# Grouped-query attention on one core: the first K and Q heads as 32-bit loads on SyncE's and ScalarE's queues, GpSimd's correction from job 0 on

## The chip, the cores and the metric

The kernel runs on one core of a Trainium2 chip. The metric is the device time of one execution in microseconds. A core has TensorE (PE; its weight loads are listed apart as PEld), VectorE (DVE), ScalarE (ACT), GpSimd (POOL) and SyncE (SP). The engines run side by side, each in the order of its own instruction list, and wait for each other through semaphores. A transfer is issued on the queue of SP, ACT or POOL and moved by 16 DMA engines. TensorE writes to PSUM, from which VectorE and ScalarE read.

## The reference

Q is 8 x 512 x 32 x 64 (batch, sequence, heads, dimension), K and V are 8 x 512 x 8 x 64, all fp32. Four query heads share one K and one V head.

```python
scores = np.einsum('bhqd,bhkd->bhqk', Q, K_expanded) * scale      # scale = 1/sqrt(64)
weights = np.exp(scores - np.max(scores, axis=-1, keepdims=True))
weights = weights / (np.sum(weights, axis=-1, keepdims=True) + 1e-10)
output = np.einsum('bhqk,bhkd->bhqd', weights, V_expanded)
```

## The kernel before

The work is 64 jobs. A *unit* u is one batch and one pair of K heads (32 units, 8 query heads each); a *job* j is one of the two K heads of a unit (g = j % 2) with its four query heads, taken as two pairs i = 0, 1. Two heads of a pair stand in the lower and the upper 64 partitions (m = 0, 1), so one transpose of 128 x 128 turns two heads at once.

Per job the scores are computed transposed, keys in the partitions and the 512 queries along the row, in 16 blocks (i, kc, m). ScalarE takes 14 of them in seven tiles of two (13 in the wide jobs, even ones from 8 on): two matmuls into a PSUM tile `s_ps` (two buffers), then one `activation(Exp)` into `pt` (`act_tile`, L220 to L228). The remaining two blocks (three) go to VectorE through the PSUM tile `d_ps` (one buffer): `u` is the linear part of an exponential made of bits (L237), `f` masks its fraction (L258), `g` and `w` are a correction (`correction`, L248), and the sum of u and w is written into `pt` (`exp_d4`, L268). `by_pool(j)` says who computes g and w: VectorE for jobs 0 to 2 and the last one, GpSimd for the others. Where GpSimd does it, `exp_d4` comes one job later.

While job j's scores run, the output of job j - 1 is computed: 64 matmuls with `pt` as weights into the PSUM tile `pv` (one buffer; `pv`, L287), first pair i = 0, then i = 1. A column of ones in V gives the row sums. VectorE takes the reciprocal and writes `o_sb` (`norm`, L330), which frees `pv`. SyncE stores a unit's output.

Q is loaded by GpSimd's queue, which rounds fp32 to bf16 on the way, into `q_nat` (four buffers). It is transposed on TensorE against an identity (`trans_q`, L165) into `d_ps` and copied to `qt` by VectorE. K of batches 1 to 7 is transposed by DMA (`dma_k`, on SyncE's queue, issued in the code at job 4 of the batch before). K of batch 0 is transposed on TensorE (`first_k`, L136) and copied to `kt_first`. Of each pair of K heads there are two versions, the heads in order and swapped (`swap`), so that each head is at hand in both halves of the partitions. The plain version takes four transposes and the swapped one eight.

The order is written out by hand (`tc.manual_schedule`): each engine executes its instructions in the order of the code. At the start (L395 to L417) GpSimd issues K heads 0 and 1, then Q of unit 0 in three pieces, builds the identity, and issues the rest of batch 0. TensorE runs eight warm-up matmuls, the twelve transposes of K's first pair in both versions into one `d_ps` tile, and then the first Q transposes into the next `d_ps` tile. In every job behind the fourth score tile, TensorE makes the Q transposes for a later job and, in batch 0, those of a later K pair; the copies come behind them on VectorE (`reads`, L463 to L488). At job 1 GpSimd waits for part of job 0's `pt` (`gate`, L429) before it issues the Q loads of units 2 and 3.

Of the kernel before, what the change touches and what calls it, by code (L numbers as in the profile page):

```python
# [11 lines left out]
FP32 = mybir.dt.float32  # L12
BF16 = mybir.dt.bfloat16
# [45 lines left out]
def fast_path(ctx, tc, Q, K, V, out, flag):  # L59
    nc = tc.nc  # L60
    B, S, H, D = Q.shape
    KV = K.shape[2]
    HPG = H // KV
    SC = S // 128
# [8 lines left out]
    const_pool = ctx.enter_context(tc.tile_pool(name="const", bufs=1))  # L73
    qnat_pool = ctx.enter_context(tc.tile_pool(name="qnat", bufs=4))
# [9 lines left out]
    s_pool = ctx.enter_context(tc.tile_pool(name="sps", bufs=2, space=PS))  # L84
    d_pool = ctx.enter_context(tc.tile_pool(name="dps", bufs=1, space=PS))
    pv_pool = ctx.enter_context(tc.tile_pool(name="pv", bufs=1, space=PS))

    ident = const_pool.tile([128, 128], BF16, name="ident")
    ok = const_pool.tile([128, SPB * 2 * SC], FP32, name="ok")
# [4 lines left out]
    ones = const_pool.tile([128, 1], BF16, name="ones")  # L94
    kt_first = const_pool.tile([128, GP, 2, S], BF16, name="kt_first")
    vt = [const_pool.tile([128, SC, KV, D + 1], BF16, name=f"v{j}") for j in range(2)]

    kn, qn, kt, qt = {}, {}, {}, {}

    def load_k(b, lo=0, hi=KV):  # L100
        if b not in kn:
            kn[b] = knat_pool.tile([128, SC, KV, D], BF16, name="k_nat")
        nc.gpsimd.dma_start(
            out=kn[b][:, :, lo:hi, :],
            in_=K[b, :, lo:hi, :].rearrange("(sc p) g d -> p sc g d", p=128),
        )


    def load_v(b, lo=0, hi=KV, chunks=range(SC)):
        for sc in chunks:  # L110
            nc.gpsimd.dma_start(  # L111
                out=vt[b % 2][:, sc, lo:hi, 0:D],
                in_=V[b, sc * 128:(sc + 1) * 128, lo:hi, :],
            )

    def load_v_head(b, g):
        nc.gpsimd.dma_start(
            out=vt[b % 2][:, :, g, 0:D], in_=V[b, :, g, :].rearrange("(sc p) d -> p sc d", p=128)
        )

    def load_q(u, cuts=(0, 2 * HPG)):
        b, gp = divmod(u, GP)
        h0 = gp * 2 * HPG
        qn[u] = qnat_pool.tile([128, SC, 2 * HPG, D], BF16, name="q_nat")
        for lo, hi in zip(cuts[:-1], cuts[1:]):
            nc.gpsimd.dma_start(  # L126
                out=qn[u][:, :, lo:hi, :],
                in_=Q[b, :, h0 + lo:h0 + hi, :].rearrange("(sc p) h d -> p sc h d", p=128),
            )

    def d_tile():
        return d_pool.tile([128, 2, S], FP32, name="d_ps")
# [3 lines left out]
    def first_k(gp, swap, bank):  # L136
        half_bank = bank.bitcast(BF16)[:, 0:S]
        ps = half_bank.rearrange("p (sc c) -> p sc c", sc=SC)
        h = 2 * gp
        for sc in range(SC):  # L140
            if swap:
                for half, g in ((0, 1), (64, 0)):
                    nc.tensor.transpose(ps[half:half + 64, sc, :], kn[0][:, sc, h + g, :], ident)  # L143
            else:
                nc.tensor.transpose(ps[:, sc, :], kn[0][:, sc, h:h + 2, :], ident)  # L145
        return lambda: nc.vector.tensor_copy(out=kt_first[:, gp, swap, :], in_=half_bank)  # L146

    def dma_k(b):
        kt[b] = kt_pool.tile([128, 2, GP, S], BF16, name="kt")
# [39 lines left out]
    NJOB = NU * 2  # L189
    DPAIR = NPAIR - 1  # L190

    def taken(j):
        return 3 if WIDE(j) else 2
# [10 lines left out]
    def scores(j, ps, i, kc, m):  # L204
        u, g = divmod(j, 2)
        b, gp = divmod(u, GP)
        keys = kt_first[:, gp, :, :] if b == 0 else kt[b][:, :, gp, :]
        return nc.tensor.matmul(  # L208
            ps,
            keys[64 * m:64 * m + 64, g ^ m, kc * 128:(kc + 1) * 128],  # L210
            qt[u][64 * m:64 * m + 64, g, i, :],
            start=True,
            stop=True,
        )

    def open_job(j):
        pt = pt_pool.tile([128, NPAIR, SC, 2, S], FP16, name="pt")
        jobs.setdefault(j, {}).update(pt=pt, pv={})

    def act_tile(j, n, spare=None):  # L220
        group = act_tiles(j)[n]
        i, kc, lo = group[0]
        ps = s_pool.tile([128, 2, S], FP32, name="s_ps") if spare is None else spare
        for _, _, m in group:
            scores(j, ps[:, m, :], i, kc, m)
        return nc.scalar.activation(  # L226
            out=jobs[j]["pt"][:, i, kc, lo:, :], in_=ps[:, lo:, :], func=EXP, scale=scale
        )  # L228
# [12 lines left out]


    def by_pool(j):
        return 3 <= j < NJOB - 1

# [16 lines left out]
    def exp_d3(j, engine):  # L264
        st = jobs[j]
        correction(engine, st["f"], st["g"], st["w"])
# [125 lines left out]
        )  # L392


    load_k(0, 0, 2)  # L395
    load_q(0, (0, 2, 4, 8))
    make_identity(nc, ident)
    nc.gpsimd.memset(ones, 1.0)
    nc.gpsimd.memset(ok, 1.0)
    for j in range(2):  # L400
        nc.gpsimd.memset(vt[j][:, :, :, D:D + 1], 1.0)
    load_v_head(0, 0)
    load_k(0, 2, 4)
    load_q(1)
    load_v_head(0, 1)
    load_k(0, 4, KV)
    load_v(0, 2, KV)


    nc.vector.memset(warm, 0.0)  # L410
    bank = d_tile()
    for j in range(8):
        nc.tensor.matmul(bank[:, 1, :], warm[:, 0:128], warm, start=True, stop=True)
    for read in [first_k(0, swap, bank[:, swap, :]) for swap in range(2)]:
        read()
    bank = d_tile()
    trans_q(0, bank[:, 0, :], 0, 1)()  # L417


    for j in range(NJOB):  # L420
        end = j == NJOB - 1
        last = j - 1
        late = last >= 0
        u, g = divmod(j, 2)
        b, gp = divmod(u, GP)
        open_job(j)
        if j == 1:

            nc.gpsimd.tensor_copy(out=gate, in_=jobs[0]["pt"][0:1, 0, SC - 1, 0, 0:1])  # L429
            load_q(2)  # L430
            load_q(3)
        if g == 0 and u >= 1 and u + 3 < NU:
            load_q(u + 3)
        if (gp, g) == (1, 0) and b + 1 < B:
            load_k(b + 1)
        if 3 <= 2 * gp + g < 3 + SC and b + 1 < B:
            load_v(b + 1, chunks=(2 * gp + g - 3,))
        if gp == 2 and g == 0 and b + 1 < B:
            dma_k(b + 1)

        cut = (4, 18) if taken(j) > 2 else (11, 19)
        act_tile(j, 0)
        if j == 0:
            trans_q(0, bank[:, 1, :], 1, NPAIR)()
            act_tile(j, 1)
            exp_d(j, 0, 2, d_tile())()
        else:
            exp_d(j, 0, 2, d_tile())()
            act_tile(j, 1)

        if j == 8:
            check_v(0, 0)
        if g == (b < B - 1) and j > 1:
            check_v(b, gp)
        if late:
            pv(last, 0, 0, 16)
        act_tile(j, 2)
        if late:
            pv(last, 0, 16, 32)
            norm(last, 0)  # L460
        act_tile(j, 3)

        reads = []  # L463
        if not end:
            bank = d_tile()
            beside = act_tile(j, 4, bank) if taken(j) > 2 else None

            ahead = (j + 1,) if j < 6 else (7, 8) if j == 6 else (j + 2,)
            for n, to in enumerate(ahead):
                if to < NJOB:  # L470
                    reads.append(trans_q(to, bank[:, n, :], other=beside))
            if j == 1:
                for swap in range(2):
                    reads.append(first_k(1, swap, bank[:, 1, swap * S // 2:]))
            elif j > 1 and b == 0 and gp + 1 < GP:
                reads.append(first_k(gp + 1, g, bank[:, 1, :]))
        else:
            pv(j, 0, 0, 16)
        copies = [] if by_pool(j) else [read() for read in reads]
        if late and by_pool(last):  # L480
            exp_d4(last)
        check_sums()
        exp_d2(j)
        if not by_pool(j):
            exp_d3(j, nc.vector)
            exp_d4(j)
        else:
            copies = [read() for read in reads]  # L488
        if taken(j) == 2:
            act_tile(j, 4)  # L490
        if late:
            pv(last, 1, 0, cut[0])
        act_tile(j, 5)
        if not end and taken(j + 1) > 2:
            exp_d(j + 1, 2, taken(j + 1), bank[:, 1:2, :], copies[0])()
        if late:
            pv(last, 1, *cut)
        act_tile(j, 6)
        if late:
            pv(last, 1, cut[1], 32)  # L500
            norm(last, 1)
            del jobs[last]
        if end:
            pv(j, 0, 16, 32)
            norm(j, 0)
            pv(j, 1, 0, 32)
            norm(j, 1)
# [118 lines left out]
```

## Time and profile before

| | |
|---|---|
| time, median of 3 runs | 420.73 us (420.61 to 420.81) |
| profiled execution | 421.54 us, of which the span from first to last instruction is 419.8 us |
| ScalarE busy | 401.3 us (96%) |
| TensorE busy | 381.2 us (91%), mean granted clock 0.992 |
| VectorE busy | 345.0 us (82%) |
| GpSimd busy | 293.4 us (70%) |

A timeline row gives the start and the length in us, the engine, the line (L12 is line 12 of the kernel), the operation, what it writes and reads, and how many instructions were merged; in brackets stand the engine's idle time in front and what released it. A group row gives the busy time, the mean of one in ns, and the idle time in front with its releasers. A row of windows gives the busy time of each engine in one stretch.

### The profile page before, as it was taken

What the parts mean: (1) busy time and instruction counts of PE and PEld (TensorE: products, weight loads), DVE (VectorE), ACT (ScalarE), POOL (GpSimd) and SP (SyncE); (2) the same over time, 40 slices, a digit from 0 to 9 for tenths busy, and PEclk for the clock granted to TensorE, in tenths of its full rate; (3) what the DMA queues carried; (4) which work ended last, traced back from release to release, by engine and by line L of the source; (5) the groups of instructions that cost most, each with busy time, mean ns of one, the idle gap of its engine ahead of it and who ended that gap; (6) DMA issues with size and microseconds to landing.
All of it is one profiled execution on the core that took longest, in us unless ns stands there. A gap on an engine that the chain in (4) does not pass through costs nothing.

```text
span 419.8 us, 13065 instructions
## 1 busy us (share of the span) xinstructions
PE 381.2 (91%) x5689; PEld 235.2 (56%) x5689; DVE 345.0 (82%) x612; ACT 401.3 (96%) x449; POOL 293.4 (70%) x209
## 2 busy tenths in 40 slices
PE   7888999999999999999999999999999999999983
PEld 2455565565565556556555556555655655555652
DVE  1687888888888888888888888888889888898875
ACT  2889999999999999999999999999999999999992
POOL 8504757788758876788867887687886887667550
PEclk9899999999999999999999999999999999999998
DMA  9996985599967998499964999659986899732223
GB/s 97 175 143 161 194 188 127 88 204 181 209 152 108 208 198 163 133 205 126 236 145 123 213 152 258 160 77 202 200 178 151 141 189 209 157 115 101 103 101 106
DMA packets 91438, 66.95 MB, mean 159 GB/s; under 512 B 52080, under 2 KB 74608, under 8 KB 91376
## 3 DMA queue, kind: packets, MB, share of 16 engines
q0 software_dynamic: 56544, 25.17, 51.6%
q1 hardware_dynamic: 34832, 40.90, 34.6%
q8 instruction: 45, 0.74, 0.7%
q14 instruction: 17, 0.14, 0.1%
HBM read 50.33 MB, written 33.55 MB: 200 GB/s over the span
## 4 chain that ended last, share of the span: by engine, by line
ACT 80%; PE 12%; DVE 5%; issue 1%; POOL 1%; ACTq 0%; DVEq 0%; POOLq 0%
ACT pt L226 80%; PE s_ps L208 6%; PE pv L302 3%; PE d_ps L172 1%; DVE o_sb L349 1%; DVE pt L271 1%; DVE qt L176 1%; DVE w L254 1%; POOL q_nat L126 0%; DVE u L237 0%; DVE kt_first L146 0%; PE d_ps L143 0%; DVE f L258 0%; DVE g L250 0%; PE d_ps L145 0%
## 5 line engine op out<-in xcount | busy, mean ns | idle before, releaser
L226 ACT ACTIVATE pt<-s_ps 128x1024 f16<-128x1024 f32 x420 | 398.1, 1284 | 9.7 <-PE s_ps L208 9.5
L302 PEld LDWEIGHTS <-pt 128*128 128x128 f16 x4096 | 142.6, 98 | 77.5 <-issue 56.3
L302 PE MATMUL pv<-v,pt 128*128 128x65 bf16 x4032 | 178.8, 195 | 2.4 <-DVE o_sb L349 1.9
L208 PE MATMUL s_ps<-qt,kt 64*128 64x512 bf16 x728 | 142.6, 383 | 22.4 <-ACT pt L226 16.3
L254 POOL TENSOR_TENSOR w<-g,f 128x1024 bf16<-128x1024 bf16 (+1 forms) x60 | 154.7, 2578 | 5.0
L250 POOL TENSOR_SCALAR g<-f 128x1024 bf16<-128x1024 int16 (+1 forms) x60 | 74.5, 1241 | 105.6 <-DVE f L258 105.6
L237 DVE TENSOR_SCALAR u<-d_ps 128x1024 int16<-128x1024 f32 (+1 forms) x92 | 96.8, 1052 | 0.7 <-PE d_ps L208 0.7
L349 DVE TENSOR_TENSOR o_sb<-pv,inv 128x512 f32<-128x512 f32 x125 | 86.4, 691 | 4.3
L208 PEld LDWEIGHTS <-kt 64*128 64x128 bf16 x896 | 51.8, 93 | 62.3 <-issue 35.0
L345 DVE RECIPROCAL inv<-pv 128x8 f32<-128x8 f32 x125 | 25.9, 207 | 54.1 <-PE pv L302 54.1
L271 DVE TENSOR_TENSOR pt<-u,w 128x1536 uint16<-128x1536 int16 (+1 forms) x64 | 51.1, 799 | 0.2
L176 DVE COPY qt<-d_ps 128x1024 bf16<-128x1024 bf16 (+1 forms) x65 | 43.9, 676 | 4.3 <-PE d_ps L172 3.1
L208 PE MATMUL d_ps<-qt,kt 64*128 64x512 bf16 x168 | 43.0, 375 | 0.0
L172 PE MATMUL d_ps<-ident,q_nat 128*128 128x128 bf16 x512 | 40.7, 224 | 1.1 <-DVE kt_first L146 0.9
L172 PEld LDWEIGHTS <-q_nat 128*128 128x128 bf16 x512 | 29.6, 99 | 21.5 <-issue 21.4
L258 DVE TENSOR_SCALAR f<-u 128x1536 int16<-128x1536 int16 (+1 forms) x64 | 30.9, 482 | 0.0
L111 POOL DMA_DIRECT2D v<-in_V_dram x32 | 29.0, 910 | 0.5 <-issue 0.5
L126 POOL DMA_DIRECT2D q_nat<-in_Q_dram x34 | 27.4, 806 | 1.4 <-DMA q_nat<-in_Q_dram 1.2
L208 PE MATMUL s_ps<-qt,kt_first 64*128 64x512 bf16 x112 | 23.4, 413 | 4.5 <-ACT pt L226 3.5
L226 ACT ACTIVATE pt<-d_ps 128x512 f16<-128x512 f32 x28 | 25.2, 899 | 0.0
L182 DVE TENSOR_REDUCE okv<-v 128x1 f32<-128x512 bf16 x32 | 21.6, 675 | 0.0
L208 PEld LDWEIGHTS <-kt_first 64*128 64x128 bf16 x128 | 7.8, 95 | 12.3 <-issue 8.6
(41 smaller groups left out, 45.5 us busy)
## 6 DMA issues: line engine op xcount, KB each, us to landing
out_dram<-o_sb SPq DMA_DIRECT2D x31, 1024.0 KB, 6.5
q_nat<-in_Q_dram POOLq DMA_DIRECT2D x31, 512.0 KB, 5.9
k_nat<-in_K_dram POOLq DMA_DIRECT2D x7, 512.0 KB, 8.3
v<-in_V_dram POOLq DMA_DIRECT2D x28, 128.0 KB, 7.8
kt<-kt SPq DMA_DIRECT2D x14, 256.0 KB, 4.4
out_dram<-o_sb SPq DMA_DIRECT2D x4, 256.0 KB, 2.4
kt<-k_nat SPq DMA_TRANSPOSE x28, 5.7
v<-in_V_dram POOLq DMA_DIRECT2D x4, 96.0 KB, 8.7
```

The costliest lines, as they stand in the source:

```text
L111: nc.gpsimd.dma_start(out=vt[b % 2][:, sc, lo:hi, 0:D], in_=V[b, sc * 128:(sc + 1) * 128, lo:hi, :],)
L172: nc.tensor.transpose(ps[:, i, sc, :], qn[u][:, sc, h:h + 2, :], ident), other
L176: return lambda: apart(nc.vector.tensor_copy(out=qt[u][:, g, lo:hi, :], in_=ps[:, lo:hi, :, :].rearrange("p i sc c -> p i (sc c)")), other)
L208: return nc.tensor.matmul(ps, keys[64 * m:64 * m + 64, g ^ m, kc * 128:(kc + 1) * 128], qt[u][64 * m:64 * m + 64, g, i, :], start=True, st ...
L226: return nc.scalar.activation(out=jobs[j]["pt"][:, i, kc, lo:, :], in_=ps[:, lo:, :], func=EXP, scale=scale)
L237: return lambda: nc.vector.tensor_scalar(out=st["u"][:, lo:hi, :], in0=ps[:, 0:hi - lo, :], scalar1=A_U, scalar2=B_U, op0=ALU.mult, op1=AL ...
L250: engine.tensor_scalar(out=g, in0=f, scalar1=-EXP_F1, scalar2=EXP_K * 2.0 ** (24 * as_bits), op0=ALU.add, op1=ALU.mult,)
L254: engine.tensor_tensor(out=w, in0=g, in1=f.bitcast(FP16) if as_bits else f, op=ALU.mult)
L258: nc.vector.tensor_single_scalar(out=st["f"], in_=st["u"], scalar=1023, op=ALU.bitwise_and)
L271: nc.vector.tensor_tensor(out=st["pt"][:, DPAIR, :, :, :].rearrange("p kc m q -> p (kc m) q")[:, 0:n, :].bitcast(U16), in0=st["u"], in1=st ...
L302: nc.tensor.matmul(st["pv"][i][:, m, qc, :], st["pt"][:, i, kc, m, qc * 128:(qc + 1) * 128], vt[b % 2][:, kc, 2 * gp + g, :], start=(n < 2 ...
L349: nc.vector.tensor_tensor(out=osb[u][:, :, h:h + 2, :].rearrange("p qc m d -> p m qc d"), in0=sums[:, :, :, 0:D], in1=inv[:, :, :, None].t ...
```

## The change

K heads 0 and 1 and the first two Q heads no longer come through GpSimd's queue. K heads 0 and 1 are loaded as fp32, one transfer each, on SyncE's queue (`key_head`), and Q heads 0 and 1 as fp32 on ScalarE's. VectorE rounds them: `first_keys` copies one K head to bf16 twice side by side (`twice`), so that four transposes give this head in both halves of the partitions; Q heads go to their place in `q_nat`. For unit 0 the score matmuls therefore take version g in both halves. K head 0 is turned at the start and K head 1 in job 0.

GpSimd's list begins with the identity, then the other Q heads of unit 0, V, and the rest; two memsets go to its end. `load_q` takes a range of heads instead of a list of cuts.

The warm-up is four matmuls instead of eight, in an `s_ps` tile; the first Q transposes go to a `pv` tile instead of `d_ps`, and so do those made in job 0. The twelve transposes of the second K pair, all made in job 1 before, are divided: the swapped version in job 1, the plain one at the end of job 0, into the `pv` tile. `by_pool` now holds for jobs 0 to 2 as well, so that GpSimd computes their g and w, and their `exp_d4` comes one job later.

```diff
+    kf = [const_pool.tile([128, SC, D], FP32, name=f"kf{g}") for g in range(2)]
+    qf = const_pool.tile([128, SC, 2, D], FP32, name="qf")
...
+    def first_keys(g, bank):
+        twice = const_pool.tile([128, SC, 2, D], BF16, name=f"twice{g}")
+        nc.vector.tensor_copy(
+            out=twice, in_=kf[g][:, :, None, :].to_broadcast((128, SC, 2, D))
+        )
+        half_bank = bank.bitcast(BF16)[:, 0:S]
+        for sc in range(SC):
+            nc.tensor.transpose(half_bank[:, sc * 128:(sc + 1) * 128], twice[:, sc, :, :], ident)
+        return lambda: nc.vector.tensor_copy(out=kt_first[:, 0, g, :], in_=half_bank)
...
-            keys[64 * m:64 * m + 64, g ^ m, kc * 128:(kc + 1) * 128],
+            keys[64 * m:64 * m + 64, g if u == 0 else g ^ m, kc * 128:(kc + 1) * 128],
...
-        return 3 <= j < NJOB - 1
+        return j < NJOB - 1
...
-    load_k(0, 0, 2)
-    load_q(0, (0, 2, 4, 8))
+    def pv_tile():
+        return pv_pool.tile([128, 2, S], FP32, name="pv")
+
+    def s_tile():
+        return s_pool.tile([128, 2, S], FP32, name="s_ps")
+
+    def key_head(g):
+        nc.sync.dma_start(out=kf[g], in_=K[0, :, g, :].rearrange("(sc p) d -> p sc d", p=128))
+
+    key_head(0)
+    nc.scalar.dma_start(out=qf, in_=Q[0, :, 0:2, :].rearrange("(sc p) h d -> p sc h d", p=128))
+    key_head(1)
     make_identity(nc, ident)
-    nc.gpsimd.memset(ones, 1.0)
-    nc.gpsimd.memset(ok, 1.0)
+    load_q(0, 2, 4)
+    load_q(0, 4, 8)
+    load_v_head(0, 0)
     for j in range(2):
         nc.gpsimd.memset(vt[j][:, :, :, D:D + 1], 1.0)
-    load_v_head(0, 0)
...
+    nc.gpsimd.memset(ones, 1.0)
+    nc.gpsimd.memset(ok, 1.0)
 
 
     nc.vector.memset(warm, 0.0)
-    bank = d_tile()
-    for j in range(8):
+    bank = s_tile()
+    for j in range(4):
         nc.tensor.matmul(bank[:, 1, :], warm[:, 0:128], warm, start=True, stop=True)
-    for read in [first_k(0, swap, bank[:, swap, :]) for swap in range(2)]:
-        read()
-    bank = d_tile()
+    copy = first_keys(0, d_tile()[:, 0, :])
+    copy()
+    bank = pv_tile()
+    nc.vector.tensor_copy(out=qn[0][:, :, 0:2, :], in_=qf)
     trans_q(0, bank[:, 0, :], 0, 1)()
...
-            bank = d_tile()
+            bank = d_tile() if j else pv_tile()
...
-            if j == 1:
-                for swap in range(2):
-                    reads.append(first_k(1, swap, bank[:, 1, swap * S // 2:]))
+            if j == 0:
+                reads.append(first_keys(1, bank[:, 1, :]))
+            elif j == 1:
+                reads.append(first_k(1, 1, bank[:, 1, :]))
...
         act_tile(j, 6)
+        if j == 0:
+            first_k(1, 0, bank[:, 1, S // 2:])()
```

More of the change, by code (lines that the diff above doesn't have):

```diff
@@ L119, in load_v_head, with load_q @@
         )
-    def load_q(u, cuts=(0, 2 * HPG)):
+    def load_q(u, lo=0, hi=2 * HPG):
         b, gp = divmod(u, GP)
         h0 = gp * 2 * HPG
[L124 to L129, printed above, removed]
+        if u not in qn:
+            qn[u] = qnat_pool.tile([128, SC, 2 * HPG, D], BF16, name="q_nat")
+        nc.gpsimd.dma_start(
+            out=qn[u][:, :, lo:hi, :],
+            in_=Q[b, :, h0 + lo:h0 + hi, :].rearrange("(sc p) h d -> p sc h d", p=128),
+        )
     def d_tile():
@@ L146, in first_k @@
         return lambda: nc.vector.tensor_copy(out=kt_first[:, gp, swap, :], in_=half_bank)
+    def first_keys(g, bank):
+        twice = const_pool.tile([128, SC, 2, D], BF16, name=f"twice{g}")
+        nc.vector.tensor_copy(
+            out=twice, in_=kf[g][:, :, None, :].to_broadcast((128, SC, 2, D))
+        )
+        half_bank = bank.bitcast(BF16)[:, 0:S]
+        for sc in range(SC):
+            nc.tensor.transpose(half_bank[:, sc * 128:(sc + 1) * 128], twice[:, sc, :, :], ident)
+        return lambda: nc.vector.tensor_copy(out=kt_first[:, 0, g, :], in_=half_bank)
     def dma_k(b):
```

## The prediction

> **What bounds the kernel now.** I read the page first: whole-span shares, then the costliest groups.
>
> ```profile
> span 419.8 us, 13065 instructions
> PE 381.2 (91%) x5689; PEld 235.2 (56%) x5689; DVE 345.0 (82%) x612; ACT 401.3 (96%) x449; POOL 293.4 (70%) x209
> L226 ACT ACTIVATE pt<-s_ps 128x1024 f16<-128x1024 f32 x420 | 398.1, 1284 | 9.7 <-PE s_ps L208 9.5
> ```
>
> ScalarE's exponentials are the bound: 96% busy, and in front of 420 of them ScalarE idled only 9.7 us in all. The change takes no exponential away, so it can win only in that idle time. ScalarE's own timeline says where it lies.
>
> ```profile
> 9.07 4.03 ACT L226 ACTIVATE pt<-s_ps 128x1024 f16<-128x1024 f32 x4 [6.91 <-PE s_ps L208]
> 13.61 5.78 ACT L226 ACTIVATE pt<-s_ps 128x1024 f16<-128x1024 f32 x6 [0.51 <-PE s_ps L208]
> 19.91 1.02 ACT L226 ACTIVATE pt<-s_ps 128x1024 f16<-128x1024 f32 x1 [0.52 <-PE s_ps L208]
> 21.63 4.69 ACT L226 ACTIVATE pt<-s_ps 128x1024 f16<-128x1024 f32 x5 [0.70 <-PE s_ps L208]
> 26.85 6.71 ACT L226 ACTIVATE pt<-s_ps 128x1024 f16<-128x1024 f32 x7 [0.53 <-PE s_ps L208]
> 33.74 1.94 ACT L226 ACTIVATE pt<-s_ps 128x1024 f16<-128x1024 f32 x2 [0.17 <-PE s_ps L208]
> 35.87 32.28 ACT L226 ACTIVATE pt<-s_ps 128x1024 f16<-128x1024 f32 x35 [0.19 <-PE s_ps L208]
> ```
>
> First start at 9.07, then six gaps in jobs 0 to 3: 0.51 + 0.52 + 0.70 + 0.53 + 0.17 + 0.19 = 2.62 us. From 35.87 on it runs without one. So the time is (first start) + (early gaps) + a rest that the diff leaves alone, and two numbers are to be forecast. The timeline of all engines shows what makes the 9.07.
>
> ```profile
> 0.88 1.28 ACT L226 ACT_TABLE_LOAD   x1 [0.88 <-PEq L610]
> 1.40 0.95 POOL L103 DMA_DIRECT2D k_nat<-in_K_dram  x1 [0.82 <-POOLq L610]
> 2.36 2.23 POOL L126 DMA_DIRECT2D q_nat<-in_Q_dram  x3
> 4.56 0.24 POOL masks.py:197 MEMSET ident<- 128x128 bf16 x1
> 4.86 0.10 PEld L145 LDWEIGHTS <-k_nat 128*128 128x128 bf16 x1 [0.84 <-DMA k_nat<-in_K_dram]
> 4.88 0.29 POOL masks.py:199 TENSOR_SCALAR_AFFINE_SELECT ident<-ident 128x128 bf16<-128x128 bf16 x1
> 5.22 0.58 PE L145 MATMUL d_ps<-ident,k_nat 128*128 128x128 bf16 x4 [0.29 <-POOL ident masks.py:199]
> 6.42 0.76 DVE L146 COPY kt_first<-d_ps 128x512 bf16<-128x512 bf16 x2 [5.14 <-PE d_ps L143]
> 7.32 0.59 PE L172 MATMUL d_ps<-ident,q_nat 128*128 128x128 bf16 x4 [0.95 <-DVE kt_first L146]
> ```
>
> GpSimd issues four transfers (until 2.36 + 2.23 = 4.59) and only then builds the identity, ready at 5.17. K landed by 4.86. Then everything is serial: K transposes, two copies ending at 7.18, Q transposes (held back by the copies, since both sets used the one `d_ps` buffer), Q copy, scores, exponential. From the end of the copies to the first exponential is 9.07 - 7.18 = 1.89 us.
>
> **The start, costed.** Removed: three of four GpSimd issues in front of the identity go behind it and one falls away (K and the first two Q heads leave GpSimd). The identity's two steps, 4.56 to 5.17, move to about 1.4 to 2.0 and leave the path. The four warm-up matmuls taken out lay beside the loads. Added: three 32-bit transfers on the idle queues of SyncE and ScalarE, and two VectorE roundings on the path. Durations for such loads are not in the trace, so bounds from the nearest ones:
>
> ```profile
> out_dram<-o_sb SPq DMA_DIRECT2D x4, 256.0 KB, 2.4
> kt<-kt SPq DMA_DIRECT2D x14, 256.0 KB, 4.4
> 13.67 0.71 DVE L258 TENSOR_SCALAR f<-u 128x1024 int16<-128x1024 int16 x1
> ```
>
> The engines are let go at 0.88 (table load row), so an issue falls near 0.9. K head 0 (128 KB): low end 0.9 + 2.4 = 3.3, as SyncE's 256 KB store; high end 0.9 + 3.46 = 4.4, as GpSimd's K load took from 1.40 to 4.86. I take 3.6, near the store: same queue, half the bytes, but two neighbours in flight. Q (256 KB): 3.3 by the store, 5.3 by the 4.4 of the SBUF copy, 6.6 if the table load's 1.28 also stands in front of ScalarE's issue; I take 4.6. A rounding writes 512 elements; the kt_first copies of that size took 0.76 for two, so 0.4; high end 0.71, the slow f row.
>
> From K's landing: rounding 0.45 with its handover, four transposes 0.62 (the 0.58 row), one copy 0.42 in place of two, Q's rounding 0.42 (queued on VectorE behind that copy), then the 1.89: 3.8 us. That is 3.6 + 3.8 = 7.4. Q's own path is landing + 0.45 + 1.89, or 6.9 with 4.6, so K sets it. Ends: 3.3 + 3.7 = 7.0, and 6.6 + 0.7 + 1.89 = 9.2 (a late Q). **Gain at the start 1.65 us, between 2.1 and -0.1.**
>
> **The gaps, costed.** What sits in front of them:
>
> ```profile
> 10.73 1.23 DVE L237 TENSOR_SCALAR u<-d_ps 128x1024 int16<-128x1024 f32 x1 [0.70 <-PE d_ps L208]
> 12.01 1.01 PE L172 MATMUL d_ps<-ident,q_nat 128*128 128x128 bf16 x8 [0.17 <-DVE u L237]
> 16.84 0.95 PE L302 MATMUL pv<-v,pt 128*128 128x65 bf16 x16
> 20.54 0.39 PE L145 MATMUL d_ps<-ident,k_nat 128*128 128x128 bf16 x4
> 20.85 0.41 PE L143 MATMUL d_ps<-ident,k_nat 128*64 128x128 bf16 x8
> 23.03 0.43 DVE L250 TENSOR_SCALAR g<-f 128x1024 bf16<-128x1024 int16 x1
> 23.49 0.69 DVE L254 TENSOR_TENSOR w<-g,f 128x1024 bf16<-128x1024 bf16 x1
> 24.22 0.69 DVE L271 TENSOR_TENSOR pt<-u,w 128x1024 uint16<-128x1024 int16 x1
> 25.06 0.69 DVE L349 TENSOR_TENSOR o_sb<-pv,inv 128x512 f32<-128x512 f32 x1
> 25.81 0.68 PE L302 MATMUL pv<-v,pt 128*128 128x65 bf16 x16 [0.88 <-DVE o_sb L349]
> ```
>
> *Gap at 13.61.* The Q transposes of job 1 waited for u; in a pv tile they need not, and start 0.15 earlier. But K head 1's four transposes now stand between them and the next scores: 0.4 to 0.58 more. Its rounding, queued on VectorE behind u (to 11.96, plus 0.42), is done before those eight transposes are, so it costs nothing unless K head 1 is late. Gap 0.51 becomes 0.8.
>
> *Gap at 21.63.* Twelve K transposes stood there; four move to the end of job 0, where TensorE is half idle (windows below). A saving of 0.2 to 0.39: 0.70 becomes 0.4. Their copy lands on VectorE ahead of job 1's u and holds the bank that job 1's output matmuls want; I cost it at nothing because the copies otherwise end about 5 us after the first exponential and those matmuls start 7.7 after it (16.84 - 9.07). Uncovered, it is one copy, 0.4.
>
> *Gaps at 26.85, 33.74, 35.87.* TensorE at 25.81 waited 0.88 for o_sb, queued behind g, w and pt. In jobs 0 to 2 g and w (0.43 + 0.69) go to GpSimd and pt is done a job later, ahead of f. VectorE is then 1.1 us plus a K copy of 0.4 earlier, more than the 0.88. All three gaps, 0.89, close.
>
> *Gap at 19.91.* It stands in a stretch with a low granted clock:
>
> ```profile
> 3.00:4.00 1.00, 1.00 (x4) 0.43 (x3) 0.00 (x0) 0.00 (x0) 1.00 (x3) 1.00 1.03 99
> ...
> 14.00:15.00 1.00, 0.32 (x2) 0.10 (x2) 0.93 (x3) 1.00 (x2) 0.15 (x1) 1.00 1.97 166
> 15.00:16.00 1.00, 0.48 (x6) 0.20 (x4) 0.97 (x2) 1.00 (x2) 0.63 (x1) 1.00 2.19 162
> 17.00:18.00 1.00, 1.00 (x18) 0.73 (x15) 0.47 (x1) 1.00 (x2) 0.76 (x2) 0.51 1.60 191
> ...
> 20.00:21.00 1.00, 1.00 (x18) 0.90 (x18) 0.29 (x1) 0.93 (x1) 0.00 (x0) 0.79 1.26 210
> ```
>
> (Columns: length, busy us and count for PE, PEld, DVE, ACT, POOL, then the clock, the DMA share and GB/s.) About 3.4 us at half clock, after a stretch in which TensorE was 0.32 and 0.48 busy. Job 0 stays as thin, so I let the drop recur and keep 0.45. [...]
>
> Gaps after: 0.8 + 0.45 + 0.4 = 1.65, so **1.0 us gained, between 2.6 (all close) and -0.5**.
>
> **GpSimd's queue.** The cover for moving g and w:
>
> ```profile
> 9.10 3.32 POOL L111 DMA_DIRECT2D v<-in_V_dram x4
> 35.68 1.04 POOL L250 TENSOR_SCALAR g<-f 128x1024 bf16<-128x1024 int16 x1 [16.42 <-DVE f L258]
> 36.80 2.13 POOL L254 TENSOR_TENSOR w<-g,f 128x1024 bf16<-128x1024 bf16 x1
> ```
>
> It stood idle 16.42 us there. Its start-up issues, until 12.4 before, end about 10.7; f of job 0 comes near 11.3, so w is ready about 14.6 and is read in job 1 near 18.7: 4 us to spare. Behind it the loads of units 2 and 3 slip by some 2 us, and batch 1's K load, behind the second correction, from 17 to about 24; its keys are wanted at job 8, near 60. No cost. SyncE's two issues lie in front of nothing.
>
> **Sum.** 1.65 + 1.0 = 2.65. The profiled execution: span 419.8 - 2.65 = 417.15, plus 421.54 - 419.8 = 1.74 around it, 418.9. That execution lies 0.8 above the median of the three runs, so against 420.73 I forecast **418.1 us**.
>
> **Rivals.** (1) *No clock drop*: the gaps at 19.91 and 21.63 close; 418.1 - 0.85 = 417.25. [...] Against: job 0 is as thin as before.
>
> (2) *The start is not won*: three 32-bit transfers plus GpSimd's share the same DMA engines, Q lands near 6.4 and the first exponential comes at 8.8. Only 0.3 + 1.0 is won: 419.4. For it: before, the first three to four loads moved only 99 GB/s at 3 to 4 us (first row above). Against: the store's 2.4. [...] No run shows this load.
>
> (3) *Slower, by the clock*: fewer warm-up matmuls and a thinner start leave TensorE at half clock for further 3.4 us windows in jobs 1 and 2. TensorE is 91% busy, so a window at half clock leaves 3.4 x (0.91 - 0.5) = 1.4 us undone. It decides from two windows (2.8 against the 2.65); with three, 418.1 + 4.2 = 422.3. Against it: one window before.
>
> (4) *Little changes*: GpSimd is late for one of jobs 0 to 2, VectorE's pt waits for w, and o_sb, and so the output matmuls behind it, come no earlier; the 0.89 stays, and with Q late too: 419.4 + 0.9 = 420.3. Against: 4 us to spare.
>
> **How the numbers follow.** Forecast 0.43, (1) 0.24, (2) 0.16, (3) 0.08, (4) 0.09. Runs spread by 0.05%; about 0.2%, 0.84 us, can be told from no change. Faster means under 419.9: the first two, most of (2): 0.82. Within: a bit of (2) and most of (4): 0.09. Slower: (3) and a rest: 0.09. The range must leave out 0.2 at most: 416.4 (start 7.0 and the gaps of (1), with a little more) to 419.9, which takes in (2) and leaves out (3) and most of (4).
>
> **What would show it.** First exponential near 7.4, with K's rounding near 3.6; no wait of pv for o_sb in jobs 1 and 2; gap of job 0 near 0.8; a half-clock stretch of 3.4 us in job 1; GpSimd's g and w three times before 35; no gap after job 3. The forecast is wrong if Q's rounding waits past 5.5 us, if half clock lasts over 7 us, or if VectorE waits for w.

## The result and the profile after

The changed kernel takes 417.38 us (416.80 to 417.45, five runs) beside 420.61 us for the kernel before on the same chip: 3.2 us less, a ratio of 0.9916 with an interval of 0.9904 to 0.9928. The two profiled spans differ by more, 419.8 - 415.8 = 4.0 us, because the profiled execution of before, at 421.54 us, lies 0.9 us above the median of its kernel; the trace below is compared with that execution, step by step.

The page of the changed kernel:

```profile
span 415.8 us, 13054 instructions
PE 378.1 (91%) x5681; PEld 233.7 (56%) x5681; DVE 342.6 (82%) x609; ACT 400.6 (96%) x449; POOL 301.5 (73%) x213
L239 ACT ACTIVATE pt<-s_ps 128x1024 f16<-128x1024 f32 x420 | 397.4, 1289 | 6.1 <-PE s_ps L221 6.1
```

The same 420 exponentials, 96% busy, and 6.1 us of idle time in front of them instead of 9.7. ScalarE's timeline of the changed kernel, with the first exponential of job 8 that reads a `d_ps` tile as a common mark:

```profile
8.01 4.03 ACT L239 ACTIVATE pt<-s_ps 128x1024 f16<-128x1024 f32 x4 [5.34 <-PE s_ps L221]
12.76 51.53 ACT L239 ACTIVATE pt<-s_ps 128x1024 f16<-128x1024 f32 x56 [0.72 <-PE s_ps L221]
64.01 0.77 ACT L239 ACTIVATE pt<-d_ps 128x512 f16<-128x512 f32 x1
```

and the mark in the kernel before:

```profile
67.88 0.75 ACT L226 ACTIVATE pt<-d_ps 128x512 f16<-128x512 f32 x1
```

The first exponential comes at 8.01 instead of 9.07 (1.06 us). One gap is left of six, 0.72 instead of 2.62 us in sum (1.90 us). Between the first exponential and the mark, 60 tiles, lie 56.00 us instead of 58.81: 2.81 us, 0.9 more than the gaps say. A single exponential takes 1.02 us, but in an unbroken row they follow each other every (51.53 - 1.02) / 55 = 0.92 us, so every gap that closes brings about 0.1 us besides its own length, and short waits merged into the rows of before go too. 1.06 + 2.81 = 3.87 of the 4.0 us are won by that mark; behind it both kernels run alike. How much of the 1.06 belongs to the start itself depends on which execution of before was profiled (b_again below).

The start, in the changed kernel's timeline:

```profile
0.88 0.48 ACTq L418 DMA_DIRECT2D qf<-in_Q_dram  x1
0.89 1.01 SPq L415 DMA_DIRECT2D kf<-in_K_dram  x2
1.16 0.29 POOL masks.py:199 TENSOR_SCALAR_AFFINE_SELECT ident<-ident 128x128 bf16<-128x128 bf16 x1
4.03 0.41 POOL L425 MEMSET v<- 128x32 bf16 x2
4.05 0.68 DVE L153 CAST twice<-kf 128x512 bf16<-128x512 f32 x1 [2.77 <-DMA kf<-in_K_dram]
4.78 0.61 PE L158 MATMUL d_ps<-ident,twice 128*128 128x128 bf16 x4 [1.56 <-DVE twice L153]
5.43 0.42 DVE L159 COPY kt_first<-d_ps 128x512 bf16<-128x512 bf16 x1 [0.70 <-PE d_ps L158]
5.77 0.42 DVE L442 CAST q_nat<-qf 128x512 bf16<-128x512 f32 x1
6.25 0.61 PE L185 MATMUL pv<-ident,q_nat 128*128 128x128 bf16 x4 [0.85 <-DVE q_nat L442]
```

The identity is ready at 1.45. K head 0, issued at 0.89, is there at 4.03, 0.8 us earlier than K's two heads were before. What follows it is shorter: four K transposes and one copy, 4.78 to 5.85, where twelve and two took 5.22 to 7.18. VectorE's rounding of Q stands between that copy and the Q transposes.

GpSimd's correction of job 0 and VectorE's use of it, in the same timeline:

```profile
12.79 2.12 POOL L267 TENSOR_TENSOR w<-g,f 128x1024 bf16<-128x1024 bf16 x1
...
18.46 0.68 DVE L284 TENSOR_TENSOR pt<-u,w 128x1024 uint16<-128x1024 int16 x1
```

w is ready at 14.91 and read at 18.46. And the windows of job 1, with TensorE's clock in the column behind the five engines:

```profile
13.00:14.00 1.00, 0.31 (x4) 0.09 (x1) 0.24 (x1) 1.00 (x2) 1.00 (x1) 1.00 2.07 166
...
17.00:18.00 1.00, 1.00 (x21) 0.72 (x22) 0.36 (x2) 1.00 (x2) 0.00 (x0) 1.00 0.89 130
```

TensorE is as thinly busy in the microsecond from 13 us as it was from 14 us before (0.31 and 0.32), and the half clock of job 1 does not come back. The microsecond behind it is busier, though: 0.81 here, 0.48 before.

### The profile page after: what moved, and what is told of

The parts are those of the page before. It is cut to its first block, busy times and chain, and to the rows that moved or that the text cites. A ratio compares the mean times of both kernels' runs of the same rounds, so it can differ in the third digit from the quotient of the medians.

```text
span 415.8 us, 13054 instructions
## 1 busy us (share of the span) xinstructions
PE 378.1 (91%) x5681; PEld 233.7 (56%) x5681; DVE 342.6 (82%) x609; ACT 400.6 (96%) x449; POOL 301.5 (73%) x213
## 4 chain that ended last, share of the span: by engine, by line
ACT 84%; PE 10%; DVE 3%; issue 1%; DMA 1%; ACTq 0%; DVEq 0%
ACT pt L239 84%; PE s_ps L221 6%; PE pv L315 3%; DMA kf<-in_K_dram 1%; DVE o_sb L362 1%; DVE pt L284 1%; PE pv L185 1%; PE d_ps L185 1%; DVE qt L189 0%; DVE ok L326 0%; ACTq L239 0%; DVE w L267 0%; DVE f L271 0%; PE d_ps L146 0%; DVE twice L153 0%
## 5 line engine op out<-in xcount | busy, mean ns | idle before, releaser
L267 POOL TENSOR_TENSOR w<-g,f 128x1024 bf16<-128x1024 bf16 (+1 forms) x63 | 161.0, 2555 | 5.2
L263 POOL TENSOR_SCALAR g<-f 128x1024 bf16<-128x1024 int16 (+1 forms) x63 | 77.4, 1229 | 96.6 <-DVE f L271 96.6
L189 DVE COPY qt<-d_ps 128x1024 bf16<-128x1024 bf16 x62 | 42.3, 684 | 0.0
L185 PE MATMUL d_ps<-ident,q_nat 128*128 128x128 bf16 x496 | 38.3, 220 | 0.0
```

The lines of the kernel that those rows point to most:

```text
L185: nc.tensor.transpose(ps[:, i, sc, :], qn[u][:, sc, h:h + 2, :], ident), other
L189: return lambda: apart(nc.vector.tensor_copy(out=qt[u][:, g, lo:hi, :], in_=ps[:, lo:hi, :, :].rearrange("p i sc c -> p i (sc c)")), other)
L263: engine.tensor_scalar(out=g, in0=f, scalar1=-EXP_F1, scalar2=EXP_K * 2.0 ** (24 * as_bits), op0=ALU.add, op1=ALU.mult,)
L267: engine.tensor_tensor(out=w, in0=g, in1=f.bitcast(FP16) if as_bits else f, op=ALU.mult)
```

## The experiments

Each was timed beside the kernel before; that kernel's medians in the three series are 420.5, 420.8 and 420.65 us. Where tenths of a microsecond are told apart, the kernels' own runs are compared, which lie closer together than those of the kernel before. The changed kernel itself was timed once, in a series of its own, so a difference from it of 0.3 us or less, about what the kernel before moves from series to series, shows nothing by itself.

**b_again: the kernel before, once more.** No edit.

> The kernel before, run again, to see whether its stretch of half clock in job 1 belongs to it. Theory: the thin TensorE stretch of job 0 brings the drop in every execution, so each shows a mean granted clock near 0.992 and a span near 419 to 420 us. Rival: the drop is chance; then some executions show 0.996, as the changed kernel does, and are about 0.9 us shorter.

Measured: 420.79 us (419.9 to 421.65). The spans are of two kinds, 418.3 to 419.1 us with a mean clock of 0.982 to 0.988, and 419.8 to 419.9 us with 0.992 to 0.996. This time one of the first kind was profiled. Its windows and its timeline:

```profile
8.00:9.00 1.00, 1.00 (x8) 0.43 (x8) 0.24 (x1) 0.57 (x1) 1.00 (x2) 1.00 1.64 148
...
10.00:11.00 1.00, 0.86 (x4) 0.15 (x2) 1.00 (x1) 1.00 (x2) 1.00 (x2) 0.50 1.19 183
...
19.00:20.00 1.00, 1.00 (x14) 0.70 (x12) 0.74 (x2) 0.62 (x1) 0.00 (x0) 0.81 1.24 206
```

```profile
5.74 0.41 PE L143 MATMUL d_ps<-ident,k_nat 128*64 128x128 bf16 x8
7.10 0.38 PE L172 MATMUL d_ps<-ident,q_nat 128*128 128x128 bf16 x4 [0.94 <-DVE kt_first L146]
9.61 1.41 PE L208 MATMUL s_ps<-qt,kt_first 64*128 64x512 bf16 x4
...
8.43 3.82 ACT L226 ACTIVATE pt<-s_ps 128x1024 f16<-128x1024 f32 x4 [6.26 <-PE s_ps L208]
```

Both expectations fall. Four Q transposes take 0.38 here and took 0.59 in the first profile, and the eight K transposes at 5.74 take 0.41 and took 0.64: TensorE ran at full clock between about 5.7 and 9.1, ahead of the first exponential, which comes at 8.43 instead of 9.07; then at half clock (0.50 in the column) for ten microseconds. The lower mean clock belongs to the *shorter* executions. In the first profile TensorE was slow through the whole start, and the clock column said 1.00 there, up to its fall at 17.01. So in these profiles only the matmuls' durations tell the clock of the start: in b_again two score matmuls take 0.61 us where the column reads 0.50 (at 13.83) and 0.39 us where it reads 1.00 again (at 20.42). Against this execution the changed kernel gains only 0.42 us at the start (8.43 - 8.01) and 2.66 us from there to the mark, which stands at 67.09 here.

**e_dve: g and w of jobs 0 to 2 back on VectorE.**

```diff
-        return j < NJOB - 1
+        return 3 <= j < NJOB - 1
```

> The changed kernel with g and w of jobs 0 to 2 back on VectorE. Theory: o_sb of jobs 1 and 2 is again queued behind g, w and pt, TensorE's output matmuls wait for it (0.3 to 0.9 us), and 0.5 to 0.9 us of gaps come back in jobs 2 and 3: about 418.1 us. Rival (the clock closed the gaps, not GpSimd): no gap comes back at full clock, 417.4 us.

Measured: 418.48 us (418.42 to 418.49), 1.1 us over the changed kernel and more than the 0.7 expected. ScalarE's and VectorE's timelines of this kernel:

```profile
16.96 1.94 ACT L239 ACTIVATE pt<-s_ps 128x1024 f16<-128x1024 f32 x2 [0.21 <-PE s_ps L221]
19.09 4.69 ACT L239 ACTIVATE pt<-s_ps 128x1024 f16<-128x1024 f32 x5 [0.20 <-PE s_ps L221]
23.98 6.71 ACT L239 ACTIVATE pt<-s_ps 128x1024 f16<-128x1024 f32 x7 [0.20 <-PE s_ps L221]
30.87 1.94 ACT L239 ACTIVATE pt<-s_ps 128x1024 f16<-128x1024 f32 x2 [0.18 <-PE s_ps L221]
33.00 32.28 ACT L239 ACTIVATE pt<-s_ps 128x1024 f16<-128x1024 f32 x35 [0.19 <-PE s_ps L221]
```

```profile
21.35 0.69 DVE L284 TENSOR_TENSOR pt<-u,w 128x1024 uint16<-128x1024 int16 x1
...
22.20 0.69 DVE L362 TENSOR_TENSOR o_sb<-pv,inv 128x512 f32<-128x512 f32 x1
```

Five gaps of about 0.2 us are back, at a clock column of 1.00 from 8 to 22 us, with o_sb behind pt on VectorE again. The theory holds, and not the clock, for the three gaps of jobs 2 and 3: TensorE waits 0.55 us for o_sb ahead of them, at 22.95 and at 29.85. The two of job 1 are of another kind: there TensorE waited 0.58 us, at 15.94, for the copy of the second K pair, which was itself queued behind g, w and pt. And the gap of job 0 is absent in this profile: between 12 and 13 us TensorE is busy for 0.41 us in it and for the whole microsecond in the changed kernel's, so job 0's transposes and the scores behind them were done sooner. So the 1.0 us by which the mark comes later (65.02) is the five gaps less that one.

**e_pool: this edit alone, in the kernel before.**

```diff
-        return 3 <= j < NJOB - 1
+        return j < NJOB - 1
```

> The kernel before with one edit of the change: g and w of jobs 0 to 2 on GpSimd. Theory: worth the same 1.1 us here as its undoing cost in the changed kernel, by the gaps in front of jobs 2, 3 and 4 that waited for o_sb: 419.5 us against 420.6. Rival: without the earlier start of GpSimd's queue w is late, VectorE waits for it and less than half is won.

Measured: 419.48 us (419.12 to 420.75) beside 420.65, ratio 0.9978 (0.9963 to 0.9992): 1.2 us by the medians, as expected, and 0.9 by the ratio. ScalarE's timeline:

```profile
17.87 2.17 ACT L226 ACTIVATE pt<-s_ps 128x1024 f16<-128x1024 f32 x2 [0.41 <-PE s_ps L208]
20.46 45.11 ACT L226 ACTIVATE pt<-s_ps 128x1024 f16<-128x1024 f32 x49 [0.42 <-PE s_ps L208]
```

No gap is left behind 20.46; the three that waited for o_sb are closed by this edit alone. So is one of job 1's, which b_again had at 20.86 (0.45).

**e_gpq: the three 32-bit loads on GpSimd's queue.**

```diff
-        nc.sync.dma_start(out=kf[g], ...
+        nc.gpsimd.dma_start(out=kf[g], ...
...
-    nc.scalar.dma_start(out=qf, ...
+    nc.gpsimd.dma_start(out=qf, ...
```

> The changed kernel with the three 32-bit loads issued on GpSimd's queue, in the same place and order ahead of the identity. Theory (the queues are what the start won): K head 0 lands near 4.8 as GpSimd's K load did before and Q about 1 us later, the first exponential comes near 8.8 instead of 8.0: about 418.2 us. Rival (the DMA engines set the landing, whoever issues): K lands at 4.0 as now and the time stays at 417.4 us.

Measured: 417.60 us (417.53 to 417.85), 0.2 us over the changed kernel. Its timeline:

```profile
1.42 0.95 POOL L415 DMA_DIRECT2D kf<-in_K_dram  x1 [0.84 <-POOLq L639]
...
4.17 0.43 DVE L153 CAST twice<-kf 128x512 bf16<-128x512 f32 x1 [2.89 <-DMA kf<-in_K_dram]
...
4.80 0.58 PE L158 MATMUL d_ps<-ident,twice 128*128 128x128 bf16 x4 [1.58 <-POOL ident masks.py:199]
...
5.76 0.71 DVE L442 CAST q_nat<-qf 128x512 bf16<-128x512 f32 x1
...
8.29 2.11 ACT L239 ACTIVATE pt<-s_ps 128x1024 f16<-128x1024 f32 x2 [6.13 <-PE s_ps L221]
...
64.00 0.77 ACT L239 ACTIVATE pt<-d_ps 128x512 f16<-128x512 f32 x1
```

The rival holds: K head 0 is there for VectorE at 4.17 instead of 4.05 although it is issued half a microsecond later, and TensorE turns it at 4.80 instead of 4.78. The first exponential comes 0.28 us later, but behind those transposes, because Q's rounding took 0.71 us instead of 0.42. By the mark nothing of it is left, 64.00 against 64.01: the gap of job 0 is 0.42 instead of 0.72 in this profile. So no gain of the new queues is shown; the 0.2 us between the times is within what the series differ by. That leaves less work as what won the start: one K head of 32 bits ahead of everything, four transposes and one copy. This is argued; those were not tried one by one.

**e_ktog: all twelve transposes of the second K pair in job 1.**

```diff
-                reads.append(first_k(1, 1, bank[:, 1, :]))
+                for swap in range(2):
+                    reads.append(first_k(1, swap, bank[:, 1, swap * S // 2:]))
...
-        if j == 0:
-            first_k(1, 0, bank[:, 1, S // 2:])()
```

> The changed kernel with all twelve transposes of the second K pair in job 1 again. Theory: four transposes, 0.2 to 0.39 us, and one copy return to the place behind job 1's fourth score tile; at full clock the score tiles in flight cover them, at half clock a gap of 0.3 to 0.7 returns: 417.4 to 418 us. If taking them out of job 0's end thins TensorE there enough to bring the clock drop back, the granted clock shows it near 17 us and the time is 418.2 us or more.

Measured: 417.62 us (416.92 to 418.79); its runs overlap those of the changed kernel, so this part is worth 0.2 us, if anything. The profiled execution keeps the clock column at 1.00 from 8 to 22 us: the drop stays away without the four transposes at the end of job 0 as well. One of the six runs, though, took 418.79 us at a mean clock of 0.993 against 0.996 to 0.998 for the others, as it could with a drop; it has no trace.

**e_warm8: eight warm-up matmuls.**

```diff
-    for j in range(4):
+    for j in range(8):
```

> The changed kernel with eight warm-up matmuls again. Theory (the clock is raised by the work of the first 5 us, in some executions): where it is raised, the K transposes, the Q transposes and the scores ahead of the first exponential take 0.4 us each instead of 0.6, as in the second profile of the kernel before, and the first exponential comes near 7.5 instead of 8.0; the executions fall into two groups about 0.5 us apart, the faster one near 416.9 us. Rival (the warm-up is idle filling): one group at 417.4 us, or 0.15 more because the K transposes wait for the last warm-up matmul.

Measured: 416.48 us (416.27 to 416.62), 0.9 us under the changed kernel, and one group, not two. TensorE's and ScalarE's timelines:

```profile
4.79 0.40 PE L158 MATMUL d_ps<-ident,twice 128*128 128x128 bf16 x4
7.00 0.39 PE L221 MATMUL s_ps<-qt,kt_first 64*128 64x512 bf16 x2 [0.52 <-DVE qt L189]
8.62 1.41 PE L221 MATMUL s_ps<-qt,kt_first 64*128 64x512 bf16 x4
...
7.43 3.82 ACT L239 ACTIVATE pt<-s_ps 128x1024 f16<-128x1024 f32 x4 [4.76 <-PE s_ps L221]
```

The three TensorE steps ahead of the first exponential take 0.4 instead of 0.6 each, and it comes at 7.43 instead of 8.01, as expected. At 7.8 the clock column falls to 0.50 until 11.2, and the gap of job 0 stays, with 0.53 us. The four warm-up matmuls that the change took out were worth the 0.9 us.

**e_qearly: Q's rounding ahead of the copy of K's keys.**

```diff
     copy = first_keys(0, d_tile()[:, 0, :])
+    nc.vector.tensor_copy(out=qn[0][:, :, 0:2, :], in_=qf)
     copy()
     bank = pv_tile()
-    nc.vector.tensor_copy(out=qn[0][:, :, 0:2, :], in_=qf)
```

> The changed kernel with Q's rounding put ahead of the copy of K's keys on VectorE. Theory (K's path with Q's rounding queued in it sets the start): the Q transposes follow the K transposes at once, near 5.4 instead of 6.25, the first exponential comes near 7.2 instead of 8.0, and 0.7 to 0.85 us are won: 416.6 us. Rival (Q's landing sets it, or the win is given back in job 0's gap, which widens by as much): 417.4 us.

Measured: 416.46 us (415.87 to 417.15), 0.9 us under the changed kernel. TensorE's and ScalarE's timelines:

```profile
5.32 0.61 PE L185 MATMUL pv<-ident,q_nat 128*128 128x128 bf16 x4
9.80 0.76 PE L185 MATMUL pv<-ident,q_nat 128*128 128x128 bf16 x8
...
7.09 55.58 ACT L239 ACTIVATE pt<-s_ps 128x1024 f16<-128x1024 f32 x60 [4.42 <-PE s_ps L221]
```

The theory holds: the Q transposes start at 5.32 and the first exponential comes at 7.09. The median's 0.9 us is the earlier start. In this profile, the fastest of the runs, the gap of job 0 is gone as well, because the clock rose during job 0's transposes (0.76 us for eight, against 1.03).

**e_order: job 0's fifth score tile ahead of the transposes.**

```diff
+            if j == 0:
+                act_tile(j, 4)
             bank = d_tile() if j else pv_tile()
...
-        if taken(j) == 2:
+        if taken(j) == 2 and j:
             act_tile(j, 4)
```

> The changed kernel with job 0's fifth score tile put ahead of the Q transposes and of K head 1's. Theory (the gap of 0.72 us in job 0 is these twelve transposes in front of the scores): the gap before the fifth tile goes, and some 0.4 us of it returns before the sixth, because the transposes take 1.66 us at half clock: 417.0 us. Rival (the gap is u on VectorE): nothing changes, 417.4 us.

Measured: 417.67 us (416.61 to 417.98): nothing won. ScalarE's and TensorE's timelines:

```profile
8.01 4.95 ACT L239 ACTIVATE pt<-s_ps 128x1024 f16<-128x1024 f32 x5 [5.34 <-PE s_ps L221]
13.77 50.81 ACT L239 ACTIVATE pt<-s_ps 128x1024 f16<-128x1024 f32 x55 [0.81 <-PE s_ps L221]
...
11.72 1.04 PE L185 MATMUL pv<-ident,q_nat 128*128 128x128 bf16 x8
```

The gap is the transposes, as the theory said, but it moved whole from the fifth tile to the sixth (0.81): the slow transposes, 1.04 us for eight, which run with K head 1's four from 11.72 to 13.18, and the scores behind them are not covered by the tiles in flight, wherever they stand. Where the clock rose earlier, as in e_qearly's profile (0.76 us for the eight), there is no gap: in these profiles it takes both the transposes and the half clock.

**e_both: both of these edits.**

> Both of the two edits before. If they are independent, 0.8 and 0.4 us add up: 416.2 us. If the earlier start only moves the wait to job 0's sixth tile, no better than the first of them, 416.6 us.

Measured: 416.65 us (416.57 to 416.95): no better than Q's earlier rounding alone. The gap of 0.81 us stands before the sixth tile again.

**e_memset: GpSimd's memsets away from K's rounding.**

```diff
     make_identity(nc, ident)
+    for j in range(2):
+        nc.gpsimd.memset(vt[j][:, :, :, D:D + 1], 1.0)
     load_q(0, 2, 4)
     load_q(0, 4, 8)
     load_v_head(0, 0)
-    for j in range(2):
-        nc.gpsimd.memset(vt[j][:, :, :, D:D + 1], 1.0)
```

> The changed kernel with GpSimd's two memsets into V put right behind the identity, away from K's rounding. Theory (the rounding of K head 0 takes 0.68 us instead of 0.42 because it runs beside these memsets, which start 0.02 us before it): it takes 0.42 us, the first exponential comes near 7.75 and about 0.25 us are won: 417.1 us. Rival (it is the landing transfers or GpSimd's issues that slow it): 0.68 us again, 417.4 us.

Measured: 416.58 us (416.41 to 417.87). VectorE's and ScalarE's timelines:

```profile
4.06 0.43 DVE L153 CAST twice<-kf 128x512 bf16<-128x512 f32 x1 [2.78 <-DMA kf<-in_K_dram]
...
7.77 55.57 ACT L239 ACTIVATE pt<-s_ps 128x1024 f16<-128x1024 f32 x60 [5.11 <-PE s_ps L221]
```

The rounding takes 0.43 instead of 0.68 and the first exponential comes 0.24 us earlier, as expected. The time fell by more, 0.8 us in the median, with a wide spread; in the profile the gap of job 0 is gone because the clock rose earlier (0.66 us for job 0's eight transposes, against 1.03). No run shows that this part is the memsets' doing.

**e_best and e_best2: Q's rounding first and eight warm-up matmuls; then the memsets' move as well.**

> The changed kernel with Q's rounding ahead of the copy of K's keys and eight warm-up matmuls. If the two wins (0.9 us each) are of different work, the first exponential comes near 6.6 and the time is 415.7 us. If both only remove the same gap of job 0, 416.4 us, as either alone.

> The same two edits and the memsets behind the identity: 0.25 us less than without the memsets' move if K's rounding is on the path (415.4 us), no less if it is not.

Measured: 415.44 us (414.97 to 415.46) and 415.34 us (415.25 to 415.36), ratios to the kernel before 0.9876 and 0.9877 (both 0.985 to 0.990). VectorE's, TensorE's and ScalarE's timelines of e_best2:

```profile
4.12 0.43 DVE L153 CAST twice<-kf 128x512 bf16<-128x512 f32 x1 [2.85 <-DMA kf<-in_K_dram]
4.72 0.43 PE L158 MATMUL d_ps<-ident,twice 128*128 128x128 bf16 x4
6.85 0.40 PE L185 MATMUL pv<-ident,q_nat 128*128 128x128 bf16 x4 [0.39 <-DMA q_nat<-in_Q_dram]
6.50 55.64 ACT L239 ACTIVATE pt<-s_ps 128x1024 f16<-128x1024 f32 x60 [3.83 <-PE s_ps L221]
```

The first exponential comes at 6.50 and no long gap is left. In the profile of e_best the clock rose only near 6.9 (four transposes take 0.61 us at 5.31 and 0.40 at 6.94) and the first exponential came at 7.05, later than expected, with no gap either. Of the 0.55 us between the two starts only 0.17 is left at the mark (61.88 and 62.05): in e_best2 TensorE waits 0.39 us for GpSimd's load of the next Q heads. From here on that load holds the start up, too. e_best2 is 2.0 us faster than the changed kernel and 5.3 us faster than the kernel before. Moving the memsets is worth 0.1 us on top, by runs that overlap.

## Why the prediction came out

The time, 417.38, lies in the range and 0.7 us under the forecast of 418.1. It is the first rival, *no clock drop*, 417.25, that happened. That the time lies within 0.13 us of this rival is partly luck: the start won 0.6 us less than forecast, and the stretch from there to the mark 1.0 us more (2.81 against the 1.85 of that rival's gaps), because a gap costs more than its idle time. Step by step:

**The start: right in kind, 0.6 us too early.** Forecast 7.4, measured 8.01. The mis-sized terms are K's landing, 4.03 for 3.6, and the rounding, 0.68 for 0.45 with its handover, 0.73. The rest of the path, 4.78 to 8.01, is 3.2 us where the terms gave 3.35. The range given for K's landing, 3.3 to 4.4, holds it, and I chose too near to the store of 2.4 us: the load took 3.1 us, near GpSimd's 3.46. By the profile of before with the early clock (b_again) the win is 0.42 and not 1.06: the forecast took one execution's 9.07 for the kernel's. That K sets the start and not Q is right: Q's load took 3.6 us from its issue, landing near 4.5, and its rounding waited for VectorE.

**The gap of job 0: right.** Forecast 0.8, measured 0.72, and e_order shows that the transposes make it. What the forecast didn't say is that they ran at half clock, 1.03 us for eight; the profiles in which the clock rose during them, with 0.76 us (e_qearly) and 0.66 us (e_memset), have no such gap, and neither has e_dve's, where TensorE was through with them sooner.

**The gap at 19.91: the step that failed.** "Job 0 stays as thin, so I let the drop recur and keep 0.45." No drop came at job 1, in this profile nor in any other of the changed structure with four warm-up matmuls (the clock column reads 1.00 in each of their windows from 16 to 21 us), and without it the gap at 21.63, forecast 0.4, closed too. Job 0 had not stayed as thin. The step went by two microseconds of the trace of before, in which TensorE was 0.32 and 0.48 busy; in the changed kernel the two are 0.31 and 0.81, and a longer stretch shows the difference better. In the kernel before, the clock column falls to 0.50 at 17.01 and is back at 1.00 from 20.42, after 3.41 us. The stretch of that length ahead of the fall, and the least busy one of that length in the changed kernel between 9 and 25 us:

```profile
13.60:17.01 3.41, 1.76 (x16) 0.57 (x14) 3.31 (x6) 3.40 (x4) 2.02 (x3) 1.00 2.03 166
```

```profile
13.05:16.46 3.41, 2.22 (x30) 1.18 (x27) 1.68 (x3) 3.41 (x5) 3.41 (x4) 1.00 1.89 131
```

TensorE was busy for 1.76 us before and for 2.22 us after, 0.52 and 0.65 of the stretch; the ends of matmuls are modelled, so both are rough. That this difference kept the drop away is my reading of two traces; no run was made to test it.

What begins a half-clock stretch and what ends it is not shown. It lasted 3.4 us in the kernel before (17.01 to 20.42), 10.2 in b_again (9.1 to 19.4) and 3.4 in e_warm8 (7.8 to 11.2). The first two are executions of one kernel, so part of what a given execution gets is chance.

**The gaps behind it: right.** All three closed. e_dve and e_pool price GpSimd's part at 1.1 and 1.2 us, where the step said 0.89: the step left out the extra 0.1 us that each gap costs, and the gaps of job 1 that come and go with the same edit.

**"The four warm-up matmuls taken out lay beside the loads": wrong.** They lay beside the loads, but they were not free: with eight, the start is 0.58 us shorter (e_warm8). The clock in the prediction's quoted windows at the start reads 1.00, and I took TensorE to be at full clock there; the transposes at 0.59 us in the rows I quoted, 0.40 in e_warm8, said otherwise.

**GpSimd's queue: right.** w at 14.91 (forecast 14.6), read at 18.46 (18.7); the K load of batch 1 at 23.58 (24).

**The other rivals.** (2) did not happen: Q landed near 4.5 and not near 6.4. Issuing all three loads from GpSimd cost 0.2 us by the times and nothing by the mark (e_gpq). (3) did not happen as written: no half clock showed in jobs 1 and 2. But with four warm-up matmuls TensorE was at half clock through the start (0.61 us for four transposes), and with eight it was not (0.40, e_warm8), which is worth 0.9 us; e_best, with eight as well, still had 0.61 until 5.9. (4) did not happen.

## What to carry to other kernels

Where one engine is busy all the time, count its start and its gaps, and add to each gap the pipelining that is lost when it stands alone (0.1 us each here). Read TensorE's clock at the start of a trace from the durations of like matmuls (0.61 us or 0.40 for four transposes here, at 1.00 in the column) and not from the clock column alone, and price warm-up matmuls by the steps that they speed up. What made the load early here was most likely to put little and the right thing first; which engine issues it mattered least (K head 0 at VectorE at 4.05 or 4.17).

## What the runs showed of the hardware that I had not expected

The clock column reads 1.00 in the start whether four transposes take 0.59 us (half clock; the kernel before, at 7.32) or 0.40 (e_warm8, at 6.09). The kernel before has executions of two lengths, near 418.7 and 420 us of span, and those with the lower mean clock in the column are the shorter ones; the one of them that was profiled, b_again, had full clock ahead of the first exponential (0.38 us for four transposes), where the column reads 1.00 in either kind. One further execution took 417.2 us at 0.992 and has no trace. In job 1 the clock fell behind 3.41 us in which TensorE was busy for 1.76 us (the kernel before, 13.60 to 17.01) and stayed up behind 2.22 us (the changed kernel, 13.05 to 16.46), though both have a microsecond as thin as 0.32 and 0.31; what decides it is not shown. VectorE's rounding of 512 elements took 0.42 us with no memset beside it (Q's, at 5.77) and 0.68 beside GpSimd's memsets that started with it (K's, at 4.05); in e_gpq, with no memset near, the rounding of Q took 0.71, so the memsets are not the only cause.
